# A three-block model on one NeuronCore: delta rule solved by blocks of 64 tokens, pairs of heads taken by turns, zero-filled keys

## The chip, the cores and the metric

The kernel runs on 1 core of one Trainium2 chip. The metric is the device time of one execution in microseconds; lower is better. Everything is float32, batch 1, 256 tokens, model width 2048.

## The reference, cut to what matters

Three blocks run one after the other on the same 256 tokens: gated convolution with linear attention and memory attention; sparse attention with gating and a feed-forward layer; latent attention (MLA) beside a two-way delta rule (RWKV-7). The change touches three places, the index scores of block 2 and both branches of block 3:

```python
# block 2: index scores, 8 heads of 64, one key head for all of them
s = jnp.einsum('bqhd,bsd->bqhs', qib, ki32)
score = jnp.einsum('bqh,bqhs->bqs', wib * idx_scale, jax.nn.relu(s))

# block 3, MLA: 8 heads, 128 columns of their own and 64 rotary ones, the rotary key shared
s = (jnp.einsum('bqhd,bkhd->bhqk', qn_b, k_nope)
     + jnp.einsum('bqhr,bkr->bhqk', qr_b, k_rope))

# block 3, delta rule: 16 heads of 64, forwards and backwards (d), token by token
sa = jnp.einsum('dbhij,dbhj->dbhi', st, a_t)
st = st * w_t[..., None, :] + sa[..., None] * b_t[..., None, :] + v_t[..., None] * k_t[..., None, :]
y = jnp.einsum('dbhij,dbhj->dbhi', st, r_t)
```

## The kernel before, in words

**The stream.** All large weights come from HBM as one stream of items of 128x512 numbers. `run_stream` (L476) goes through them in order. For each item ScalarE rounds the raw weights to `wh` (float32r), VectorE takes the rest, `wl = raw - wh`, and TensorE adds three products (`wh*xh`, `wl*xh`, `wh*xl`) for each half of the tokens into the two PSUM tiles `acc0` and `acc1`: six matmuls of 512 columns an item, or twelve of 256. The split runs five items ahead (`LEAD`).

**The side work.** All else (attention, delta rule, norms, transposes) is written as generators, which `pump` (L425) steps between the stream's matmuls; what TensorE makes for them goes into four further PSUM banks, called `bank` in the rows. A clock inside the builder, `Issue` (L261), has a fixed cost for each instruction; with it `pump` decides at build time after which stream matmul the next step of a generator stands. On the chip each engine then goes through its list in that order, and a TensorE instruction that must wait holds up the whole stream. All instructions pass through one recording line, so rows of the profile read L285, and are told apart by tile names.

**Narrow matmuls.** Heads are 64 wide, so two heads lie one above the other in the 128 partitions. A matmul for one head contracts over 64 partitions (rows `64*128`), and the solver below works on squares of 32 tokens (rows `32*32`, with an explicit `tile_position`). The stream and most side work contract over all 128 (rows `128*128`). A float32 matmul outside the stream stands as two records in the trace.

**Block 2, index scores.** `ev_ki` (L1555) has the key, 64 wide, doubled side by side and transposed into `kiT`, so that it lies in both halves; `indexer` (L1566) makes 8 steps of two matmuls of 64 rows.

**Block 3, MLA.** `ev_kr` (L1959) does the same with the rotary key `krT`. `mla_block` (L2026) adds for each head a product over 128 rows (`qn`, `kn`) and one over 64 rows (both in the slot `ropes`): 16 such pairs in all, each with the narrow matmul behind the full one.

**Block 3, delta rule.** Two jobs, `job(0)` and then `job(1)` (L2191), with 8 heads each; the second starts when the first has been solved. Per job and direction d, with the tokens in two blocks b of 128:
- `scores` (L2445): a matrix per head and block, `ab`, from `bk` and `ar`, 64 rows each; four matmuls a step, all of the same half of the partitions.
- `products` (L2467): 32 steps, each with one head, block and direction: one matmul of 128 columns and one of 256, 64 rows each. VectorE masks the results, and every second step TensorE multiplies three of them with the values (tile `vy`), 128 rows.
- `inverses` (L2517): the 32x32 blocks on the diagonal of `ab` go through DRAM into another layout, VectorE inverts 128 of them at a time, and they come back as `tl`.
- `solve` (L2581): for each of two blocks n, four stages e of 32 tokens, both directions together: 16 matmuls with the inverses (`bank<-w,tl`), ScalarE copies to `w0`, then the later tokens' rows of `ab` times the result (`bank<-w,ab`; 48, 32 and 16 matmuls for e = 0, 1, 2, the first two in two steps each), and VectorE adds. 40 steps and 640 matmuls over both jobs.
- `outputs` (L2689): the last reads (`bank<-w,m`), a norm per head on VectorE and ScalarE, and for the second job the transposes (`bank<-cst,vy`) that give the stream's next matrix, `br1`, its left operand.

Of the kernel before, what the change touches and what calls it, by code (L numbers as in the profile page):

```python
# [15 lines left out]
ALU = mybir.AluOpType  # L16
# [623 lines left out]
class Kernel(Builder):  # L640
# [866 lines left out]
    def block2(self):  # L1507
        nc, B = self.nc, self
        V, A, T, G = nc.vector, nc.scalar, nc.tensor, nc.gpsimd
        cv = self.cv  # L1510
        S = {}
# [24 lines left out]
        def to_T(e, dst, flag, n=4):  # L1536
# [8 lines left out]
            B.flag(flag)  # L1545

        def ev_qi(j, acc):
            S["qi_s"] = B.slot([128, 2048], name="qi")
            S["qiT"] = S["qi_s"][:, :1024].rearrange("p (c t) -> p c t", t=256)
            S["kiT"] = S["qi_s"][:, 1024:1280].rearrange("p (c t) -> p c t", t=256)  # L1550
            S["sc"] = S["qi_s"][:, 1280:1792].rearrange("p (b t) -> p b t", t=256)
            B.scaled(S["qiT"], acc, "Rb2")
            B.flag_then("qiT")

        def ev_ki(j, acc):  # L1555
            e = B.work([128, 256], "nar", 1).rearrange("p (b t) -> p b t", b=2)
            for i in range(2):
                ev_copy(e, acc, 64, 64 * i)
            for b in range(2):
                V.tensor_scalar(out=wi[:, b], in0=acc[b][:, 64:72], scalar1=R[:, b:b + 1], scalar2=512.0 ** -0.5,  # L1560
                                op0=ALU.mult, op1=ALU.mult)
            B.side(to_T(e, S["kiT"], "kiT", 1), True)
            B.side(bias())
            B.side(indexer())

        def indexer():  # L1566
# [3 lines left out]
            for h0 in (0, 4, 1, 5):  # L1570
                p0 = 64 * (h0 % 2)
# [321 lines left out]
    def block3(self):  # L1893
# [3 lines left out]
        S = {}  # L1897
# [61 lines left out]
        def ev_kr(j, acc):  # L1959
            d = B.work([128, 256], "nar", 1).rearrange("p (b t) -> p b t", b=2)  # L1960
            ev_copy(d, acc, R, 64)
            S["qrT"] = S["ropes"][:, :1024].rearrange("p (c t) -> p c t", t=256)
            S["krT"] = S["ropes"][:, 1024:1280].rearrange("p (c t) -> p c t", t=256)

            def g():
                yield from B.lock("mix")
                for b in range(2):
                    rotary(d[:, b:b + 1, 0:64], 1, b)
                    V.tensor_copy(out=d[:, b, 64:128], in_=d[:, b, 0:64])
                B.unlock("mix")  # L1970
                yield from to_T(d, S["krT"], "krT", 1)
            B.side(g(), True)
# [53 lines left out]
        def mla_block(b, i0, mp):  # L2026
# [5 lines left out]
            for h0 in (i0, i0 + 4):  # L2032
                hs = (h0, h0 + 2)
                p0 = 64 * (h0 % 2)
# [410 lines left out]
        def scores(J, d, bk):  # L2445

            ab = J["ab"][d] = yield from B.slotw([128, 16, 128], "ab")
            av = ab.rearrange("p (h b) t -> p h b t", b=2)
            for b in (0, 1) if d == 0 else (1, 0):
                for h0 in range(2):  # L2450
                    ps, = yield from B.bank()
                    for i in range(4):
                        p, c, ar = at(J, d, b, 2 * i + h0)
                        T.matmul(ps[:, i * 128:i * 128 + 128], bk[p, 0, c, b * 128:b * 128 + 128], ar[:, 0],
                                 start=True, stop=True)
                    yield
                    A.copy(out=av[:, h0::2, b], in_=ps.rearrange("p (i t) -> p i t", t=128))
                    B.unbank(ps)
            J["bk"][d] = bk
# [7 lines left out]
        def products(J):  # L2467


            masks = [B.masks[:, d * 256:d * 256 + 256] for d in range(2)]  # L2470
            seq = [(b, h, d) for b in range(2) for h in range(8) for d in range(2)]
            pend, ready = deque(), deque()
            wy, ms, rb = None, [None, None], [None, None]
            for step in range(35):
                if pend:
                    b, h, d, ps = pend.popleft()
                    m = ms[d] = B.work([128, 2, 128], f"m{d}", 3)
                    if h % 2 == 0:
                        rb[d] = B.work([128, 2, 128], f"rb{d}", 2)
                    V.tensor_tensor(out=m.rearrange("p a t -> p (a t)"), in0=ps[:, :256], in1=masks[d], op=ALU.mult)  # L2480
                    V.tensor_tensor(out=rb[d][:, h % 2], in0=ps[:, 256:384], in1=masks[d][:, :128], op=ALU.mult)
                    B.unbank(ps)
                    if h % 2:
                        B.store(J["rbd"][d][:, 8 * b + h - 1:8 * b + h + 1], rb[d])
                    if d:
                        V.tensor_tensor(out=ms[0][:, 0], in0=ms[0][:, 0], in1=m[:, 0], op=ALU.add)
                        ready.append((step, b, h, ms[0], m))
                out = None
                if ready and ready[0][0] < step:
                    _, b, h, m0, m1 = ready.popleft()  # L2490
                    if h % 2 == 0:
                        wy, = yield from B.bank()
                    vs = J["V"][:, b, h * 64:h * 64 + 64]
                    for i, l in enumerate((m0[:, 0], m0[:, 1], m1[:, 1])):
                        o = i * 128 + h % 2 * 64
                        T.matmul(wy[:, o:o + 64], l, vs, start=True, stop=True)
                    if h % 2:
                        out = wy, b, (h - 1) * 64
                if step < 32:
                    b, h, d = seq[step]  # L2500
                    ps, = yield from B.bank()
                    p, c, ar = at(J, d, b, h)
# [3 lines left out]
                    pend.append((b, h, d, ps))  # L2506
                yield
# [9 lines left out]
        def inverses(J):  # L2517
# [54 lines left out]
            for d in (1, 0):  # L2572
                for q in range(4):
                    nc.sync.dma_start(out=ts[32 * q:32 * q + 32, d], in_=td2[d, :, q].rearrange("u c t -> c u t"))
            yield
            V.transpose(out=tb[:, 1], in_=ts[:, 1])
            B.free(tmp)
            J["tt"] = [ts[:, 0], tb[:, 1]]
            B.flag(f"inv{g}")

        def solve(J):  # L2581


            for d in range(2):
                yield from B.wait(f"zb{d}{J['g']}")
            ab, tt, w0, zb = J["ab"], J["tt"], J["w0"], J["zb"]
            pw = yield from B.bank(2)
            hs = [slice(h * 64, h * 64 + 64) for h in range(8)]
            for n in range(2):
                bs = (n, 1 - n)  # L2590
                if n:
                    for c in range(4):
                        for d in range(2):
                            T.matmul(pw[d][:, c * 128:c * 128 + 128], J["ar"][1][:, d, c, 0], zb[d][:, c], start=c == 0,
                                     stop=False, skip_group_check=True)
                for e in range(4):
                    qs = (e, 3 - e)
                    rows = [slice(32 * q, 32 * q + 32) for q in qs]
                    ws = [w0[rows[d], d, bs[d]] for d in range(2)]
# [14 lines left out]

                    for h in range(8 if e < 3 else 0):
                        if h == 4 and e < 2:
                            yield
                        for i in range(e + 1, 4):
                            for d in range(2):
                                t0 = 32 * (i, 3 - i)[d]  # L2620
                                T.matmul(pw[d][t0:t0 + 32, hs[h]], ab[d][rows[d], 2 * h + bs[d], t0:t0 + 32],
                                         ws[d][:, hs[h]], start=not n and e == 0 and h == 0, stop=e == 2,
                                         tile_position=(32 * qs[d], t0), skip_group_check=True)
                if n == 0:
# [361 lines left out]
```

## Time and profile before

| | |
|---|---|
| runs | 3606.69 us median of 3 (3601.64 to 3608.61) |
| the profiled execution | 3603.35 us, its span on the core 3601.6 us |
| granted TensorE clock | 0.995 |
| busy: TensorE, VectorE, ScalarE, GpSimd | 99%, 68%, 53%, 4% |
| chain that ended last | TensorE 97% |

TensorE is the engine that is never free: its matmuls are pipelined, so what one costs is read from the start of one to the start of the next, and not from its duration. A side step costs the stream the time by which the matmuls of the stream on both sides of it stand further apart than without it.

### The profile page before, as it was taken

How to read it: one execution, taken by the hardware profiler on the slowest of the kernel's cores; microseconds unless marked ns; L12 is line 12 of the kernel's file. 1: busy time of each engine (PE TensorE's matmuls, PEld its weight loads, DVE VectorE, ACT ScalarE, POOL GpSimd, SP SyncE). 2: the span in 40 equal slices, each digit the busy share in tenths (PEclk: the TensorE clock that was granted, in tenths of full speed). 3: DMA queues.
4: the chain of work that ended last, by engine and by line, in shares of the span. 5: the costliest groups of instructions: out<-in, count | busy, mean ns of one | idle time of the engine just before them, and what ended most of it. 6: DMA issues, size and time to landing. Idle time of an engine off the chain costs nothing.

```text
span 3601.6 us, 56526 instructions
## 1 busy us (share of the span) xinstructions
PE 3561.6 (99%) x20754; PEld 3063.9 (85%) x20754; DVE 2451.2 (68%) x4453; ACT 1896.3 (53%) x3402; POOL 149.0 (4%) x141
## 2 busy tenths in 40 slices
PE   8999999999999999999999999999999999999988
PEld 7889988888988899888879898989888987887767
DVE  7598888886576665555866555555665688587675
ACT  6555556656554545655455544444564653463334
POOL 1000010010000000000200000000000010000000
PEclk9999999999999999999999999999999999999999
DMA  6555556676677765566665555555663655555655
GB/s 236 169 188 157 182 169 197 208 224 187 195 226 222 239 201 179 187 216 217 232 210 182 191 187 190 188 188 187 198 206 115 196 189 182 193 192 170 199 177 186
DMA packets 231774, 698.51 MB, mean 194 GB/s; under 512 B 40708, under 2 KB 51124, under 8 KB 229832
## 3 DMA queue, kind: packets, MB, share of 16 engines
q1 hardware_dynamic: 231496, 694.90, 59.9%
q8 instruction: 162, 2.65, 0.3%
q14 instruction: 116, 0.95, 0.1%
HBM read 661.22 MB, written 36.73 MB: 194 GB/s over the span
## 4 chain that ended last, share of the span: by engine, by line
PE 97%; DVE 1%; DMA 1%; ACT 0%; issue 0%; SPq 0%; DVEq 0%; ACTq 0%
PE acc L285 87%; PE bank L285 10%; DVE wl L285 0%; DMA raw<-in_wstream_dram 0%; DMA x<-f 0%; ACT wh L285 0%; DVE vy L285 0%; DVE o L285 0%; DVE xl L285 0%; DVE rsz L285 0%; ACT junk L285 0%; DVE yst L285 0%; ACT xh L285 0%; DVE x L285 0%; SPq L285 0%
## 5 line engine op out<-in xcount | busy, mean ns | idle before, releaser
L285 DVE TENSOR_TENSOR wl<-raw,wh 128x512 fp32r<-128x512 f32 x2290 | 1569.6, 701 | 1037.1 <-ACT wh L285 1021.4
L285 ACT ACTIVATE wh<-raw 128x512 fp32r<-128x512 f32 x2290 | 1424.3, 629 | 1529.5 <-PE acc L285 975.8
L285 PE MATMUL acc<-wh,xh 128*128 128x512 f32 x3328 | 1327.0, 399 | 7.3 <-ACT xh L285 4.4
L285 PE MATMUL acc<-wh,xl 128*128 128x512 f32 x3328 | 1298.0, 390 | 3.4 <-DVE xl L285 3.4
L285 PE MATMUL acc<-wl,xh 128*128 128x512 f32 x3328 | 1297.1, 390 | 0.0
L285 PEld LDWEIGHTS acc<-wh,xh 128*128 128x128 f32 x3328 | 626.2, 188 | 154.9 <-issue 20.6
L285 PEld LDWEIGHTS acc<-wh,xl 128*128 128x128 f32 x3328 | 626.0, 188 | 135.6 <-DVE xl L285 4.0
L285 PEld LDWEIGHTS acc<-wl,xh 128*128 128x128 f32 x3328 | 626.9, 188 | 121.8 <-DVE wl L285 0.8
L285 PE MATMUL acc<-xh,wh 128*128 128x256 f32 (+3 forms) x2224 | 638.0, 287 | 0.0
L285 PE MATMUL acc<-xh,wl 128*128 128x256 f32 (+3 forms) x2224 | 630.3, 283 | 0.0
L285 PE MATMUL acc<-xl,wh 128*128 128x256 f32 (+3 forms) x2224 | 630.2, 283 | 0.0
L285 PEld LDWEIGHTS acc<-xh,wh 128*128 128x128 f32 (+3 forms) x2224 | 424.3, 191 | 5.5 <-issue 4.0
L285 PEld LDWEIGHTS acc<-xl,wh 128*128 128x128 f32 (+3 forms) x2224 | 424.5, 191 | 1.1
L285 PEld LDWEIGHTS acc<-xh,wl 128*128 128x128 f32 (+3 forms) x2224 | 424.1, 191 | 0.3
L285 DVE SCALAR_TENSOR_TENSOR cacc<-u,cvec,cacc 128x226 f32<-128x226 f32 (+28 forms) x464 | 188.4, 467 | 0.0
L285 PE MATMUL bank<-ar,bk 64*128 64x128 f32 (+1 forms) x384 | 77.4, 328 | 0.0
L285 PEld LDWEIGHTS bank<-ar,bk 64*128 64x128 f32 x384 | 48.6, 187 | 19.2 <-issue 13.4
L285 ACT ACT_TABLE_LOAD x44 | 56.5, 1283 | 3.2 <-DVE mmx L285 1.6
L285 POOL TENSOR_TENSOR msh<-ev 128x508 f32<-128x508 f32 x8 | 10.8, 1346 | 1038.7 <-DVE ev L285 976.3
L285 ACT ACTIVATE junk<-x 128x512 bf16<-128x512 f32 x40 | 25.3, 631 | 36.7 <-DVE x L285 36.3
L285 PE MATMUL acc<-wh,yr 128*128 128x512 f32 x128 | 44.0, 408 | 0.0
L285 POOL TENSOR_TENSOR crstd<-crstd,u 128x256 f32<-128x256 f32 x14 | 21.8, 1560 | 358.6 <-DVE u L285 358.1
(420 smaller groups left out, 2223.8 us busy)
## 6 DMA issues: line engine op xcount, KB each, us to landing
raw<-in_wstream_dram SPq DMA_DIRECT2D x1133, 512.0 KB, 3.9
gate<-sg SPq DMA_DIRECT2D x40, 256.0 KB, 2.2
row<-in_rows_dram SPq DMA_DIRECT2D x38, 256.0 KB, 4.7
sg<-gate SPq DMA_DIRECT2D x24, 256.0 KB, 2.9
sg<-z SPq DMA_DIRECT2D x24, 256.0 KB, 2.6
z<-sg SPq DMA_DIRECT2D x20, 256.0 KB, 2.1
f<-x SPq DMA_DIRECT2D x16, 256.0 KB, 2.5
gt<-gate SPq DMA_DIRECT2D x16, 256.0 KB, 4.1
```

What stands on the lines that cost most here:

```text
L285: r = f(*a, **k)
```

## The change

**Keys filled with zeros (index scores, MLA).** `kiT` and `krT` now exist twice: once with the key in the upper 64 partitions and zeros in the lower, once the other way round. GpSimd writes the zeros. The matmuls take all 128 rows of the two heads' queries against the version of the head wanted.

**Heads by turns (scores, products).** A step takes two banks and works on the two heads of a pair in turn, one in the upper 64 partitions and one in the lower. `scores` has 2 steps a direction in place of 4, with 8 matmuls; `products` has 16 steps with matmuls in place of 32, with 4 in each.

**Blocks of 64 (inverses, solve).** When the inverses of 32 are back, TensorE joins two of them to one of 64: for a pair of blocks f and s, the block between them times one inverse, a copy, and that times the other. These are 128 matmuls of 32x32x32 a job, in four steps of 32, on four squares of the array by turns. The inverses are laid into `ab` itself: one direction by four further DMAs, the other by four transposes; the joined block by four ScalarE copies, the zeros opposite by GpSimd. `solve` then has two stages of 64 tokens in place of four of 32: three steps of 16 matmuls for each n, so 12 steps and 192 matmuls over both jobs.

The core of the diff:

```diff
+        def halves_T(e, dst, flag):
+            yield
+            t = yield from B.transposes([e[:, b] for b in range(2)], 128)
+            yield
+            for i in range(2):
+                V.tensor_copy(out=dst[64 * i:64 * i + 64, i], in_=t[64 * i:64 * i + 64, :256])
...
+            for i in range(2):
+                G.memset(S["kiT"][64 - 64 * i:128 - 64 * i, i], 0.0)
...
-                        T.matmul(ps[:, i * n:i * n + n], S["qiT"][p0:p0 + 64, h0 // 2 + i, b * 128:b * 128 + 128],
-                                 S["kiT"][p0:p0 + 64, 0, :n], start=True, stop=True)
+                        T.matmul(ps[:, i * n:i * n + n], S["qiT"][:, h0 // 2 + i, b * 128:b * 128 + 128],
+                                 S["kiT"][:, h0 % 2, :n], start=True, stop=True)
...
-                    T.matmul(o, S["qrT"][p0:p0 + 64, h // 2, tb], S["krT"][p0:p0 + 64, 0], start=False, stop=True)
+                    T.matmul(o, S["qrT"][:, h // 2, tb], S["krT"][h0 % 2], start=False, stop=True)
...  scores
-                for h0 in range(2):
-                    ps, = yield from B.bank()
-                    for i in range(4):
-                        p, c, ar = at(J, d, b, 2 * i + h0)
-                        T.matmul(ps[:, i * 128:i * 128 + 128], bk[p, 0, c, b * 128:b * 128 + 128], ar[:, 0],
-                                 start=True, stop=True)
+                ps = yield from B.bank(2)
+                for i in range(4):
+                    for h0 in range(2):
+                        p, c, ar = at(J, d, b, 2 * i + h0)
+                        T.matmul(ps[h0][:, i * 128:i * 128 + 128], bk[p, 0, c, b * 128:b * 128 + 128], ar[:, 0],
+                                 start=True, stop=True)
...  products
-                    T.matmul(ps[:, 256:384], J["bk"][d][p, 0, c, ts], ar[:, 1], start=True, stop=True)
-                    T.matmul(ps[:, :256], J["bk"][d][p, 1, c, ts], ar[:, ::-1], start=True, stop=True)
+                    for i, (p, _, ar) in enumerate(hs):
+                        T.matmul(ps[i][:, 256:384], J["bk"][d][p, 0, c, ts], ar[:, 1], start=True, stop=True)
+                    for i, (p, _, ar) in enumerate(hs):
+                        T.matmul(ps[i][:, :256], J["bk"][d][p, 1, c, ts], ar[:, ::-1], start=True, stop=True)
...  inverses
+            for q, qs in enumerate(qss):
+                nc.sync.dma_start(out=ab[0][qs, :, qs], in_=td2[0, :, q].rearrange("u c t -> c u t"))
...
+            for qs in qss:
+                V.transpose(out=ab[1][qs, :, qs], in_=ts[qs, 1])
+            V.transpose(out=tb[:, 0], in_=ts[:, 0])
...
+            prs = [(d, qss[2 * i + d], qss[2 * i + 1 - d], 32 * (2 * i + d), 32 * (2 * i + 1 - d))
+                   for i in range(2) for d in range(2)]
+            flipped = [tb[:, 0], ts[:, 1]]
+            zt, = yield from B.bank()
+            for u in range(16):
+                for d, f, s, tf, t2 in prs:
+                    T.matmul(zt[s, u * 32:u * 32 + 32], ab[d][f, u, s], flipped[d][f, u], start=True, stop=True,
+                             tile_position=(tf, t2), skip_group_check=True)
+                if u == 7:
+                    yield
+            yield
+            zs = tb[:, 1]
+            A.copy(out=zs.rearrange("p u t -> p (u t)"), in_=zt)
...  the second product alike, from zs and ab into zt
+            for d, f, s, _, _ in prs:
+                A.copy(out=ab[d][f, :, s], in_=zt[f].rearrange("p (u t) -> p u t", t=32))
+                G.memset(ab[d][s, :, f], 0.0)
...  solve
-                for e in range(4):
-                    qs = (e, 3 - e)
-                    rows = [slice(32 * q, 32 * q + 32) for q in qs]
+                for e in range(2):
+                    os = (64 * e, 64 - 64 * e)
+                    rows = [slice(o, o + 64) for o in os]
...
-                            T.matmul(pw[d][rows[d], hs[h]], tt[d][rows[d], 2 * h + bs[d]], ws[d][:, hs[h]], start=True,
-                                     stop=True, tile_position=(32 * qs[d], 32 * qs[d]), skip_group_check=True)
+                            T.matmul(pw[d][rows[d], hs[h]], ab[d][rows[d], 2 * h + bs[d], rows[d]], ws[d][:, hs[h]],
+                                     start=True, stop=True, tile_position=(os[d], os[d]), skip_group_check=True)
...
-                    for h in range(8 if e < 3 else 0):
...
+                    for h in range(8 if e == 0 else 0):
+                        for d in range(2):
+                            o = os[1 - d]
+                            T.matmul(pw[d][o:o + 64, hs[h]], ab[d][rows[d], 2 * h + bs[d], o:o + 64], ws[d][:, hs[h]],
+                                     start=not n, stop=True, tile_position=(os[d], o), skip_group_check=True)
```

How this moves instructions shows at three places. The first is TensorE's list in `products` of the first job; `bank_N<-ar,bk` are the products of a step, into the bank with that number. Before, one step, the stream, the next step:

```order
L285 MATMUL bank_30314<-ar,bk 128x128
L285 MATMUL bank_30314<-ar,bk 128x256
L285 MATMUL acc_30095<-wh,xh 128x512
L285 MATMUL acc_30095<-wl,xh 128x512
L285 MATMUL acc_30095<-wh,xl 128x512
L285 MATMUL bank_30331<-ar,bk 128x128
L285 MATMUL bank_30331<-ar,bk 128x256
```

Now one step, with two banks in turn:

```order
L285 MATMUL bank_30168<-ar,bk 128x128
L285 MATMUL bank_30169<-ar,bk 128x128
L285 MATMUL bank_30168<-ar,bk 128x256
L285 MATMUL bank_30169<-ar,bk 128x256
L285 MATMUL acc_30093<-wh,xh 128x512
L285 MATMUL acc_30093<-wl,xh 128x512
L285 MATMUL acc_30093<-wh,xl 128x512
```

What stood in two steps with a piece of the stream between them stands in one step.

The second place is TensorE's list at the end of the second job, from the last reads (`w,m`) to the transposes of the result (`cst,vy`). Before, 27 matmuls of the stream stand between them, of which the first and the last are shown:

```order
L285 MATMUL bank_34933<-w_32295,m_34027 128x64 x8
L285 MATMUL acc_34864<-wh,yr_33886 128x512
...
L285 MATMUL acc_34962<-wh,yr_33886 128x512
L285 MATMUL bank_35054<-cst_80,vy 128x128 x4
L285 MATMUL bank_35061<-cst_80,vy 128x128 x4
L285 MATMUL acc_35068<-wh,yr_35052 128x512
```

Now 108 matmuls of the stream stand between the reads and the first transposes, and 6 more before the second:

```order
L285 MATMUL bank_34560<-w_32123,m_34060 128x64 x8
...
L285 MATMUL acc_34821<-wh,yr_33946 128x512
L285 MATMUL bank_34844<-cst_80,vy 128x128 x4
L285 MATMUL acc_34820<-wh,yr_33946 128x512
L285 MATMUL acc_34820<-wl,yr_33946 128x512
...
L285 MATMUL bank_34861<-cst_80,vy 128x128 x4
```

The reads have moved up in the stream by 93 matmuls, and the transposes, which come just before `br1`, by 12 and by 6.

The third place is ScalarE's list at the end of `inverses` of the first job, where all is new; `wh` is the stream's split, `w` the solver's copy:

```order
L285 COPY tl<-bank_31132 128x512
L285 ACTIVATE wh<-raw 128x512
L285 COPY ab<-bank_31220 32x16x32
L285 COPY ab<-bank_31220 32x16x32 x3
L285 ACTIVATE wh<-raw 128x512
L285 COPY w_29037<-bank_31322 64x512
```

The first copy lies between the two products of the joining, the four after it between the joining and the first step of `solve`. On TensorE's list 9 matmuls of the stream cover each of the two in the first job, 9 and 12 in the second.

## Rows read from the trace of the kernel before

**Rows 1.** The page: busy time, chain by line, VectorE's largest group

```profile
PE 3561.6 (99%) x20754; PEld 3063.9 (85%) x20754; DVE 2451.2 (68%) x4453; ACT 1896.3 (53%) x3402; POOL 149.0 (4%) x141
...
PE acc L285 87%; PE bank L285 10%; DVE wl L285 0%; DMA raw<-in_wstream_dram 0%; DMA x<-f 0%; ACT wh L285 0%; DVE vy L285 0%; DVE o L285 0%; DVE xl L285 0%; DVE rsz L285 0%; ACT junk L285 0%; DVE yst L285 0%; ACT xh L285 0%; DVE x L285 0%; SPq L285 0%
...
L285 DVE TENSOR_TENSOR wl<-raw,wh 128x512 fp32r<-128x512 f32 x2290 | 1569.6, 701 | 1037.1 <-ACT wh L285 1021.4
```

**Rows 2.** TensorE's waits: who for whom, us in total, times, longest

```profile
PE bank L285 <- DVE vy L285: 16.2, 1, 16.2
```

**Rows 3.** Timeline of TensorE, a full-form step: start, us, engine, line, what

```profile
1407.22 0.28 PE L285 MATMUL acc<-xh,wl 128*128 128x256 f32 x1
1407.34 1.05 PE L285 MATMUL bank<-kv,apT 128*128 128x128 f32 x8
...
1408.34 0.28 PE L285 MATMUL acc<-xl,wh 128*128 128x256 f32 x1
```

**Rows 4.** Timeline of TensorE, a step of scores and one of products

```profile
2933.58 0.39 PE L285 MATMUL acc<-wh,xl 128*128 128x512 f32 x1
2933.90 1.16 PE L285 MATMUL bank<-ar,bk 64*128 64x128 f32 x8
...
2935.32 0.39 PE L285 MATMUL acc<-wl,xh 128*128 128x512 f32 x1
2935.55 0.40 PE L285 MATMUL acc<-wh,xl 128*128 128x512 f32 x1
...
2952.12 0.40 PE L285 MATMUL acc<-wh,xl 128*128 128x512 f32 x1
2952.45 0.92 PE L285 MATMUL bank<-ar,bk 64*128 64x128 f32 x4
...
2953.63 0.40 PE L285 MATMUL acc<-wl,xh 128*128 128x512 f32 x1
```

**Rows 5.** Timeline of TensorE, steps of solve in the first job

```profile
3066.92 0.39 PE L285 MATMUL acc<-wh,xl 128*128 128x512 f32 x1
3067.24 1.08 PE L285 MATMUL bank<-w,tl 32*32 32x64 f32 x32
...
3068.59 0.39 PE L285 MATMUL acc<-wl,xh 128*128 128x512 f32 x1
...
3071.21 0.73 PE L285 MATMUL bank<-w,ab 32*32 32x64 f32 x48
...
3081.73 0.65 PE L285 MATMUL bank<-w,ab 32*32 32x64 f32 x32
...
3090.70 1.08 PE L285 MATMUL bank<-w,ab 32*32 32x64 f32 x32
```

**Rows 6.** Timeline of TensorE, the pairs of MLA

```profile
2748.22 0.70 PE L285 MATMUL bank<-ropes 64*128 64x256 f32 x2
2748.85 0.70 PE L285 MATMUL bank<-kn,qn 128*128 128x256 f32 x2
2749.48 0.70 PE L285 MATMUL bank<-ropes 64*128 64x256 f32 x2
```

**Rows 7.** TensorE's groups by form: records, busy us, mean ns, idle before

```profile
L285 PE MATMUL bank<-ar,bk 64*128 64x128 f32 x256 | 49.6, 304 | 0.0
L285 PE MATMUL bank<-ar,bk 64*128 64x256 f32 x128 | 38.1, 377 | 0.0
```

**Rows 8.** Timeline of TensorE at the end of the second job

```profile
3448.25 3.68 PE L285 MATMUL bank<-w,m 128*128 128x64 f32 x32
3451.73 0.48 PE L285 MATMUL acc<-wh,yr 128*128 128x512 f32 x1
...
3474.50 1.94 PE L285 MATMUL bank<-cst,vy 128*128 128x128 f32 x8 [16.20 <-DVE vy L285]
```

**Rows 9.** Busy us of each engine in 44 us of products

```profile
2966.00:3010.00 44.00, 44.00 (x205) 33.70 (x204) 39.53 (x85) 17.20 (x30) 1.28 (x1) 1.00 0.59 193
```

**Rows 10.** ScalarE's groups from 3066 to 3152: the solver's copies

```profile
L285 ACT COPY w<-bank 32x512 f32<-32x512 f32 x16 | 9.2, 578 | 5.8 <-PE bank L285 5.5
```

More of the change, by code (lines that the diff above doesn't have):

```diff
@@ L1545, in to_T @@
             B.flag(flag)
+        def halves_T(e, dst, flag):
[4 more added lines that the diff above has]
+                V.tensor_copy(out=dst[64 * i:64 * i + 64, i], in_=t[64 * i:64 * i + 64, :256])
+            B.unbank(t)
+            B.flag(flag)
         def ev_qi(j, acc):
@@ L1561, in ev_ki @@
                                 op0=ALU.mult, op1=ALU.mult)
-            B.side(to_T(e, S["kiT"], "kiT", 1), True)
+            B.side(halves_T(e, S["kiT"], "kiT"), True)
             B.side(bias())
@@ L1570, in indexer @@
             for h0 in (0, 4, 1, 5):
-                p0 = 64 * (h0 % 2)
                 for b in range(2):
@@ L1962, in ev_kr @@
             S["qrT"] = S["ropes"][:, :1024].rearrange("p (c t) -> p c t", t=256)
-            S["krT"] = S["ropes"][:, 1024:1280].rearrange("p (c t) -> p c t", t=256)
+            S["krT"] = [S["ropes"][:, o:o + 256] for o in (1024, 1792)]
+            for i in range(2):
+                G.memset(S["krT"][i][64 - 64 * i:128 - 64 * i], 0.0)
             def g():
@@ L1970, in g @@
                 B.unlock("mix")
-                yield from to_T(d, S["krT"], "krT", 1)
+                yield
+                t = yield from B.transposes([d[:, b] for b in range(2)], 128)
+                yield
+                for i in range(2):
+                    V.tensor_copy(out=S["krT"][i][64 * i:64 * i + 64], in_=t[64 * i:64 * i + 64, :256])
+                B.unbank(t)
+                B.flag("krT")
             B.side(g(), True)
@@ L2470, in products @@
             masks = [B.masks[:, d * 256:d * 256 + 256] for d in range(2)]
-            seq = [(b, h, d) for b in range(2) for h in range(8) for d in range(2)]
+            seq = [(b, c, d) for b in range(2) for c in range(4) for d in range(2)]
             pend, ready = deque(), deque()
-            wy, ms, rb = None, [None, None], [None, None]
-            for step in range(35):
+            m0 = None
+            for step in range(19):
                 if pend:
[L2476 to L2484, printed above, removed]
-                    if d:
-                        V.tensor_tensor(out=ms[0][:, 0], in0=ms[0][:, 0], in1=m[:, 0], op=ALU.add)
-                        ready.append((step, b, h, ms[0], m))
@@ new lines, in products @@
+                    b, c, d, ps = pend.popleft()
+                    m = [B.work([128, 2, 128], f"m{d}{i}", 2 - d) for i in range(2)]
+                    rb = B.work([128, 2, 128], f"rb{d}", 2)
+                    for i in range(2):
+                        V.tensor_tensor(out=m[i].rearrange("p a t -> p (a t)"), in0=ps[i][:, :256], in1=masks[d], op=ALU.mult)
+                        V.tensor_tensor(out=rb[:, i], in0=ps[i][:, 256:384], in1=masks[d][:, :128], op=ALU.mult)
+                    B.unbank(*ps)
@@ L2488, in products @@
+                    B.store(J["rbd"][d][:, 8 * b + 2 * c:8 * b + 2 * c + 2], rb)
+                    if d:
+                        for i in range(2):
+                            V.tensor_tensor(out=m0[i][:, 0], in0=m0[i][:, 0], in1=m[i][:, 0], op=ALU.add)
+                        ready.append((step, b, c, m0, m))
+                    else:
+                        m0 = m
                 out = None
                 if ready and ready[0][0] < step:
-                    _, b, h, m0, m1 = ready.popleft()
@@ L2491, in products @@
[L2491 to L2502, printed above, removed]
-                    ts = slice(b * 128, b * 128 + 128)
-                    T.matmul(ps[:, 256:384], J["bk"][d][p, 0, c, ts], ar[:, 1], start=True, stop=True)
-                    T.matmul(ps[:, :256], J["bk"][d][p, 1, c, ts], ar[:, ::-1], start=True, stop=True)
-                    pend.append((b, h, d, ps))
+                    _, b, c, ms, mt = ready.popleft()
@@ new lines, in products @@
+                    wy, = yield from B.bank()
+                    for i in range(2):
+                        vs = J["V"][:, b, c * 128 + i * 64:c * 128 + i * 64 + 64]
+                        for a, l in enumerate((ms[i][:, 0], ms[i][:, 1], mt[i][:, 1])):
+                            o = a * 128 + i * 64
+                            T.matmul(wy[:, o:o + 64], l, vs, start=True, stop=True)
+                    out = wy, b, c * 128
+                if step < 16:
+                    b, c, d = seq[step]
+                    ps = yield from B.bank(2)
+                    ts = slice(b * 128, b * 128 + 128)
+                    hs = [at(J, d, b, 2 * c + i) for i in range(2)]
+                    for i, (p, _, ar) in enumerate(hs):
+                        T.matmul(ps[i][:, 256:384], J["bk"][d][p, 0, c, ts], ar[:, 1], start=True, stop=True)
+                    for i, (p, _, ar) in enumerate(hs):
+                        T.matmul(ps[i][:, :256], J["bk"][d][p, 1, c, ts], ar[:, ::-1], start=True, stop=True)
+                    pend.append((b, c, d, ps))
@@ L2585, in solve @@
                 yield from B.wait(f"zb{d}{J['g']}")
-            ab, tt, w0, zb = J["ab"], J["tt"], J["w0"], J["zb"]
+            ab, w0, zb = J["ab"], J["w0"], J["zb"]
             pw = yield from B.bank(2)
@@ L2613, in solve @@
                     yield
-                    for h in range(8 if e < 3 else 0):
[L2616 to L2623, printed above, removed]
+                    for h in range(8 if e == 0 else 0):
[3 more added lines that the diff above has]
+                                     start=not n, stop=True, tile_position=(os[d], o), skip_group_check=True)
                 if n == 0:
```

31 lines of the change are left out of this document (21 added, 10 removed).

## The prediction

> **What bounds the kernel now.** I read the page first: TensorE is busy 99% of the span, and by line the chain of waits is 87% matmuls of the stream into `acc` and 10% side work into `bank`; VectorE's largest group is the stream's split, 701 ns each [rows 1]. Then who waited for whom: TensorE's only long wait is 16.2 us, once, for VectorE's `vy` [rows 2]. So a microsecond of side work on TensorE is a microsecond of the kernel, as long as what it needs comes in time. Then the timeline, for what a side step costs the stream: from the start of the last stream matmul before it to the start of the second after it, less the two paces that would lie there anyway (0.12 us each at 256 columns, 0.23 at 512).
>
> Three readings carry the sum.
>
> *A full-form step.* Four matmuls of 128 rows and 128 columns: 1408.34 - 1407.22 - 0.24 = 0.88 us, 0.22 each, with nothing for entering or leaving [rows 3].
>
> *A narrow step.* The same four with 64 rows: 2935.32 - 2933.58 - 0.46 = 1.28, that is 0.40 more [rows 4]. The step of `products` with one matmul of 128 and one of 256 columns takes 2953.63 - 2952.12 - 0.46 = 1.05, so 0.40 + 0.22 + 0.43. The surcharge is thus paid per step, about 0.20 on each side, whatever stands in it. MLA shows it bare: full and narrow matmuls follow each other every 0.63 us [rows 6], 0.20 over the 0.43 that 256 columns take.
>
> *Squares by turns.* A step of 16 matmuls on two squares of 32x32 takes 3068.59 - 3066.92 - 0.46 = 1.21, its row's length plus 0.13 [rows 5]. Less 0.40 that is 0.81 for eight matmuls a square, 0.10 each on its own square, the other square beside it. The 24 matmuls on six squares take 0.73 + 0.13 = 0.86, less 0.40 that is 0.46 or 0.019 each; they share rows of the array and, in different banks, columns, and still run side by side. The 16 on four squares take 0.65 + 0.13 = 0.78.
>
> **The change part by part.**
>
> *Index scores.* Eight narrow steps become full: 8 x 0.40 = -3.2 us. The zeros are four GpSimd writes, here and in MLA, on an engine busy 4% [rows 1]; nothing.
>
> *MLA.* 16 pairs, two changes of form each: 32 x 0.20 = -6.4.
>
> *Scores.* Before 16 steps (128 of the records, so 64 matmuls [rows 7]) of 1.28. After, 8 steps with four matmuls in either half of the rows. I take the halves to run side by side, since squares with distinct rows and shared columns do [rows 5]: 8 x 1.28, -10.2. From above, one behind the other: 8 x (0.40 + 8 x 0.22) = 17.3, -3.2. Below the first there is nothing, for each half needs its four passes.
>
> *Products.* 64 steps of 1.05 (the other 128 records of 128 columns and the 128 of 256 [rows 7]) become 32. Side by side: -33.6. One behind the other: 32 x (0.40 + 2 x 0.65) = 54.4, -12.8. The products with the values stay 96 full matmuls.
>
> *Solve.* Before, for each of four (two jobs, two n): four steps of 1.21, two of 0.86, two of 0.78, one of 1.21 [rows 5], 9.33; together 37.3. After, 12 steps of 16 matmuls on two squares of 64x64. The moved columns are 64 as before, so I take 1.21 each: 14.5, -22.8. If the two squares did not overlap, 16 x 0.10 + 0.40 = 2.0 each, -13.3; below 1.21 a square would have to take fewer passes, which it doesn't.
>
> *Inverses.* Eight new steps of 32 matmuls on four squares, 32 columns each. No row shows 32 columns. From below half of 0.10 a matmul on its square, 8 x 0.05 + 0.40 = 0.80, together 6.4; from above all in a row at 0.10, 3.6, together 28.8. I take the pace of the six squares, 32 x 0.019 + 0.40 = 1.01, the nearest in number and kind: +8.1. The four DMAs and four transposes a job stand behind the same kind of work and before the reads of it; VectorE and the DMA queue have that time, since they finish while `products` still runs.
>
> The Trainium skill, page "TensorE: Matmul & The Clock Gate", section "Wait — 56ns, not 53.3ns?", says that matmuls start at least about 25 ns apart however few columns they have. By it an inverse step, with 64 records, would take 1.6 + 0.4 us and the eight some 16 (an estimate from that page), and the forecast would be 8 us later. The trace differs: 48 records start within 0.46 us, about 10 ns apart, on six squares [rows 5]; I go by the row.
>
> Sum on TensorE: -3.2 - 6.4 - 10.2 - 33.6 - 22.8 + 8.1 = -68.1 us.
>
> *The wait at the end of job 1.* The last reads end at 3451.73, the transposes begin at 3474.50, 22.8 us later [rows 8]. Of these 6.2 were covered by 27 stream matmuls at 0.23, the rest is the wait. In the new order 108 stand between, 24.8 us. But VectorE's list now has 13 splits and two pairs of products from `acc` among the norm's instructions, and had 4 and one pair: 9 x 0.70 [rows 1] and 2 x 0.70, 7.7 us more. So 22.8 + 7.7 - 24.8 = 5.7 us of wait stay of 16.2: -10.5. From below none stays, if VectorE works through the gaps it had; from above all 16.2.
>
> *What is late next.* After joining, four ScalarE copies at 0.58 [rows 10], 2.3 us and some latency, meet a cover of 9 matmuls (2.1 us) in job 0 and 12 in job 1; behind them stands the first step of `solve`, and the stream behind that: +0.5. In the densest stretch of `products` VectorE is busy 39.5 of 44 us [rows 9]; with ten steps in it made five, at 1.05, the stretch would be 38.7 long, below VectorE's own work: I take 2.5 us for both jobs. Together +3, from 0 to the 20 of the second rival.
>
> All: -68.1 - 10.5 + 3 = -75.6, against the profiled execution's 3603.35: 3527.8. That execution lies 3.3 below the median of the runs, 3606.69; I add half of it and forecast 3530 us.
>
> **The rivals.**
>
> *Halves one behind the other.* Two heads in the upper and lower 64 rows each use all 128 columns, which no row before shows; the squares by turns [rows 5] speak for overlap, at 32 rows only. Then scores and products save 3.2 and 12.8: TensorE -40.3, with the rest -47.8, 3556 to 3557.
>
> *VectorE takes over.* If the share of the dense stretch, 0.90 [rows 9], held from the first scores to the first step of `solve`, 2933.6 to 3067.2 [rows 4, 5], that stretch of 134 us could shrink by 13.4 and not by 21.9 (scores and products of one job): 17 us come back over two jobs, and with VectorE behind, the wait at the end keeps its 16.2. 3527.8 + 17 + 10.5 is 3555. For it: `products` brings VectorE the same masking in less time. Against it: TensorE waited for nothing there [rows 2], and the new order spreads the steps further apart.
>
> *Each turn of halves costs a change of form, and the kernel gets slower.* The surcharge of 0.20 a side [rows 6] might fall due at each turn between the two halves of the rows. There are 8 x 7 turns in scores, 32 x 3 in products, 12 x 15 in solve, 332. Nothing would overlap there: products -12.8, scores -3.2, solve -13.3, inverses +8.1, keys -9.6, -30.8; with 332 x 0.20 = +66.4 and -7.5 for the waits the kernel takes 3631. It decides from 0.12 us a turn. Against it: 16 matmuls by turns on squares with distinct rows take 0.81 us, in which 15 turns at 0.20 would be 3.0 [rows 5].
>
> **How the numbers follow.** Forecast 0.72, with a range of its own from 3515 (no wait at the end, the cheapest inverses, no new waits) to 3548 (the wait stays, dearer inverses). Halves in a row 0.12, VectorE 0.11, dear turns 0.05. To hold 8 in 10 I go up to the first two rivals: 3514 to 3558. A measurement of this kernel tells 0.2%, some 7 us, from no change. All cases but the last are far beyond that; for mixtures that eat up the gain I leave 0.02 for the same: faster 0.93, same 0.02, slower 0.05.
>
> **What would show it.** A step of `products` with four matmuls at about 1.05 us, one of `scores` with eight at 1.28; at 1.7 and 2.2 the halves take turns in earnest. A step of `solve` at 1.21, of the joining at 1.0. MLA's matmuls every 0.43. The wait for `vy` at a third of 16.2, and no wait of over 2 us between scores and solve. The forecast is wrong if these steps cost as said and TensorE's list of waits holds more than some 15 us that is new, or if the halves don't overlap.

## The result

The changed kernel takes 3540.87 us (median of 4, 3537.31 to 3546.78) against 3605.53 us before (4 runs): ratio 0.9823, 95% interval 0.9805 to 0.9841. It is 64.7 us faster; 75.6 were forecast. The time lies inside the range, 11 us above the forecast of 3530.

The profiled execution after took 3546.78 us, 5.9 above its median, and is 56.6 below the profiled one before. The page after, the busy row of its first part:

```profile
PE 3506.3 (99%) x20370; PEld 3036.2 (86%) x20370; DVE 2442.9 (69%) x4447; ACT 1893.6 (53%) x3398; POOL 158.8 (4%) x153
```

TensorE is as full as in [rows 1]. What differs stands in the list of its waits (who for whom, us in total, times, longest), against [rows 2]:

```profile
PE acc L285 <- issue: 3.6, 1, 3.6
...
PE acc L285 <- DVE yr L285: 2.0, 2, 1.8
PE bank L285 <- issue: 1.9, 2, 1.8
...
PE bank L285 <- DVE m L285: 1.3, 1, 1.3
PE bank L285 <- ACT w L285: 1.2, 1, 1.2
PE acc L285 <- DVE wl L285: 1.2, 3, 0.8
...
PE bank L285 <- DVE tl L285: 0.6, 1, 0.6
```

The one wait of 16.2 us for `vy` is gone. In its place stand eleven short ones, 11.8 us in these rows, and two lines of them have no releaser ("issue"); a further new one, 0.8 us for `qi`, stands in the index scores.

The steps themselves, from the timeline of TensorE after (start, us, engine, line, what), in order: MLA, a step of scores, one of products, one of the joining, one of solve:

```profile
2743.01 0.60 PE L285 MATMUL bank<-kn,qn 128*128 128x256 f32 x2
2743.44 0.59 PE L285 MATMUL bank<-ropes 128*128 128x256 f32 x2
...
2930.39 0.39 PE L285 MATMUL acc<-wh,xl 128*128 128x512 f32 x1
2930.71 1.16 PE L285 MATMUL bank<-ar,bk 64*128 64x128 f32 x16
...
2932.14 0.39 PE L285 MATMUL acc<-wl,xh 128*128 128x512 f32 x1
...
2943.40 0.40 PE L285 MATMUL acc<-wh,xl 128*128 128x512 f32 x1
2943.72 0.93 PE L285 MATMUL bank<-ar,bk 64*128 64x128 f32 x8
...
2944.91 0.39 PE L285 MATMUL acc<-wl,xh 128*128 128x512 f32 x1
...
3049.86 0.40 PE L285 MATMUL acc<-wh,xl 128*128 128x512 f32 x1
3050.19 0.75 PE L285 MATMUL bank<-ab,tl 32*32 32x32 f32 x64
...
3051.21 0.40 PE L285 MATMUL acc<-wl,xh 128*128 128x512 f32 x1
...
3344.21 0.39 PE L285 MATMUL acc<-wh,xl 128*128 128x512 f32 x1
3344.53 1.15 PE L285 MATMUL bank<-w,ab 64*64 64x64 f32 x32
...
3345.94 0.39 PE L285 MATMUL acc<-wl,xh 128*128 128x512 f32 x1
```

Read as in the prediction, less 0.46 or twice 0.23: scores 1.29 for eight matmuls [rows 4: 1.28 for four], products 1.05 for four (1.05 for two), joining 0.89, solve 1.27 (the median of the twelve is 1.28), MLA 0.43 a matmul [rows 6: 0.63 for a pair's turn].

**Where the microseconds stand.** Both traces have the same 17,208 matmuls of the stream in the same order. So the start of each in one trace can be set against its start in the other; the table sums by how much the time between two such marks changed, in us, for the profile after and for a second profile of the same kernel (`after_again`, run 3542.99). The last two columns belong to an experiment below.

| stretch of the stream | after | again | spread | spread again |
|---|---|---|---|---|
| parts that the change doesn't touch, up to MLA | +3.6 | +1.1 | -0.8 | +4.5 |
| index scores | -1.9 | -1.9 | -1.9 | -1.6 |
| MLA to the first scores | -4.7 | -6.2 | -6.2 | -4.7 |
| scores and products, first job | -15.5 | -15.2 | -17.6 | -17.0 |
| joining of the first job | +6.5 | +6.5 | -0.2 | 0.0 |
| solve, then the second job's scores and products | -14.9 | -16.3 | -14.0 | -11.4 |
| joining and solve, second job | -9.0 | -7.8 | -4.0 | -3.5 |
| last reads, transposes | -20.5 | -20.4 | -21.9 | -21.5 |

But for the first, the stretches repeat within some 1.5 us in the two profiles of the changed kernel (once 2.6 in the two of the spread one). The joining of the first job alone costs 6.5 us more than what stood there before, and most of that is a halt:

```profile
3051.44 0.39 PE L285 MATMUL acc<-wh,xl 128*128 128x512 f32 x1
3055.44 0.59 PE L285 MATMUL acc<-wh,xh 128*128 128x512 f32 x1 [3.60 <-issue]
3055.82 0.63 PE L285 MATMUL acc<-wl,xh 128*128 128x512 f32 x1
```

When the matmul at 3055.44 begins, TensorE has finished 2024 items of the stream and VectorE has split 2030. The split of the item that TensorE comes to is the first of these three, done at 3045.98, so its data had been there for 9 us:

```profile
3045.29 1.89 DVE L285 TENSOR_TENSOR wl<-raw,wh 128x512 fp32r<-128x512 f32 x3
```

The DMA queues in that gap, 3051.4 to 3055.4 (packets, MB, share of the 16 engines' time):

```profile
q1 hardware_dynamic: 517, 1.45, 100.6%
q8 instruction: 1, 0.02, 1.5%
```

One piece of instructions, 16 KB, moves from 3053.23 to 3054.17, beside queues that data fill. Over the whole kernel this queue moves 159 pieces for TensorE's 2 x 20370 records, one for every 256. My reading is that TensorE had come to the end of what it had loaded: just before, it went through two blocks of 256 records in 4.4 and 2.8 us, where the five before these had taken 17 to 27 us each. The piece begins to move only 1.4 us after TensorE has stopped; why so late, no run tells. And the halt has a tail. The stretches behind it, columns as in [rows 9] (PEclk is the granted clock):

```profile
3055.40:3058.10 2.70, 2.66 (x8) 1.62 (x7) 0.00 (x0) 0.00 (x0) 0.00 (x0) 0.50 1.07 408
3059.20:3062.00 2.80, 2.80 (x16) 2.33 (x13) 0.78 (x2) 1.79 (x3) 0.00 (x0) 1.00 1.02 423
```

After this halt TensorE is granted half its clock (0.50), 1.2 of 2.4 GHz: six matmuls of the stream start 0.43 apart in place of 0.23, 1.2 us more.

### The profile page after: what moved, and what is told of

It reads as the page before. It is cut to its first block, busy times and chain, and to the rows that moved or that the text cites. A ratio compares the mean times of both kernels' runs of the same rounds, so it can differ in the third digit from the quotient of the medians.

```text
span 3545.0 us, 55751 instructions
## 1 busy us (share of the span) xinstructions
PE 3506.3 (99%) x20370; PEld 3036.2 (86%) x20370; DVE 2442.9 (69%) x4447; ACT 1893.6 (53%) x3398; POOL 158.8 (4%) x153
## 4 chain that ended last, share of the span: by engine, by line
PE 91%; DVE 5%; DMA 2%; issue 1%; ACT 1%; SPq 0%; POOL 0%; DVEq 0%; ACTq 0%
PE acc L285 84%; PE bank L285 7%; DVE wl L285 2%; DVE tmp L285 1%; DMA raw<-in_wstream_dram 1%; DVE m L285 0%; ACT wh L285 0%; DMA x<-f 0%; DMA tl<-td 0%; DVE tl L285 0%; DVE rb L285 0%; ACT junk L285 0%; DVE o L285 0%; DVE xl L285 0%; DMA row<-in_rows_dram 0%
## 5 line engine op out<-in xcount | busy, mean ns | idle before, releaser
L285 PE MATMUL acc<-wh,yr 128*128 128x512 f32 x128 | 43.7, 410 | 2.0 <-DVE yr L285 2.0
L285 PE MATMUL bank<-ar,bk 64*128 64x128 f32 (+1 forms) x384 | 40.4, 329 | 0.1
L285 POOL TENSOR_TENSOR crstd<-crstd,u 128x256 f32<-128x256 f32 x14 | 21.9, 1561 | 356.5 <-DVE u L285 356.0
L285 PEld LDWEIGHTS bank<-ar,bk 64*128 64x128 f32 x384 | 25.6, 186 | 14.2 <-issue 10.0
```

The source lines that it names most:

```text
L285: r = f(*a, **k)
```

## The experiments

**One part at a time.** Each is the kernel before with one of the three parts of the diff shown above, and nothing else.

> The kernel before with the zero-filled keys alone (index scores and MLA). Theory A (every step of TensorE costs what it cost in the prediction, and what is missing of the forecast went into new short waits of the joining and the solver): eight narrow steps and 32 changes of form go, 3.2 + 6.4 = 9.6 us less, about 3596 us; in the profile MLA's matmuls follow every 0.43 us and the wait for vy at the end stays at 16.2 us. Theory B (full rows move more and the writes of zeros or the contention for SBUF eat it up): under 4 us less.

Measured: 3595.49 us against 3607.45, ratio 0.9971 (0.9960 to 0.9982), 12.0 us less, with 9.6 inside the interval. `vy` is waited for 16.2 us as before. Theory A holds.

> The kernel before with the heads by turns alone (scores and products). Theory A: scores 8 x 1.30 in place of 16 x 1.29, products 32 x 1.06 in place of 64 x 1.05, together 43.7 us less. The list of TensorE has 27 matmuls of the stream between the last reads of the second job and their transposes as before, so the wait of 16.2 us for vy stays: about 3562 us, and up to 3 more for a wait for VectorE's masks in the dense stretch. Theory B (the shorter products leave VectorE behind, and the end waits longer): the wait for vy above 20 us and 3570 us or more.

Measured: 3572.90 us, ratio 0.9907 (0.9893 to 0.9920), 34.6 us less and not 43.7. Its waits:

```profile
PE bank L285 <- DVE vy L285: 16.2, 1, 16.2
...
PE bank L285 <- DVE w L285: 2.8, 2, 2.3
```

The time is one that theory B named, but not for its reason: the wait at the end stays at 16.2, as theory A said, and the steps cost 1.05 and 1.29. But the solver's first step, still of 32, now waits for VectorE, and seven matmuls behind it run at half clock (1.4 us); seven steps of products, waiting inside for their second bank, take 1.18 to 1.71 in place of 1.05 (2.6 us together). The matmuls with the values, three before and six a step now, take 1.35 a step where two steps beside narrow ones had taken 0.62 each (16 x 0.11 = 1.8 us). 2.8 + 1.4 + 2.6 + 1.8 are 8.6 of the 9.1 us missing.

> The kernel before with the blocks of 64 alone (inverses and solve). Theory A: solve 12 x 1.28 in place of 37.4 us, -22; eight joining steps at 0.9, +7; 120 matmuls of the stream now stand between the last reads and the transposes, so the wait for vy goes, -16.2 and 2 us at half clock behind it; and TensorE stands still for some 3 to 7 us in the joining, without a releaser, while 16 KB of its instructions are fetched: -26 to -30, 3575 to 3580 us. Theory B (the stall in the joining belongs to the three parts together, to VectorE's or ScalarE's backlog): no idle time of over 1 us in the joining, -33, about 3572 us.

Measured: 3574.10 us, ratio 0.9908 (0.9894 to 0.9921), 33.3 us less. Theory B's number came true: no halt in the joining, where steps of `products` still stood among those of the joining, so that the first job's four steps take 9.0 us and not 7.0; and the wait at the end is this part's to remove, but for a rest:

```profile
PE bank L285 <- DVE vy L285: 2.7, 1, 2.7
```

The three parts alone save 12.0 + 34.6 + 33.3 = 79.9 us, together 64.7. Some 15 us are lost where they meet; by the intervals of the four ratios this difference is good to about 10 us.

**Is the halt a lack of instructions?** In the first job alone the two halves of each product of the joining are set 18 matmuls of the stream apart:

```diff
                 if u == 7:
-                    yield
+                    for _ in range(1 if g else 6):
+                        yield
```

> The changed kernel with 18 matmuls of the stream in place of 3 between the two halves of each product of the joining, in the first job alone. Theory A (TensorE ran out of fetched instructions: four steps of 128 within 8 us): the idle 3.6 us before the first step of solve and the half clock of six matmuls behind it, 1.4 us, are gone or under 1 us together, about 5 us less than the changed kernel, so 0.14% lower in its ratio to the kernel before. Theory C (the idle time is a wait that the profile doesn't name, for ScalarE's four copies or a bank): the copies stand as close before solve as they did, the idle time stays at 3 to 4 us and the time is the same within 2 us.

Measured: 3534.72 us, ratio 0.9799 (0.9786 to 0.9813). The first job's stretch went from +6.5 to -0.2 (table). In the second job, where nothing was spread, the halt stayed, and at the same place: at record 38337 of TensorE's list, as in the changed kernel, whose first-job halt is at 35009, just 13 x 256 before. The waits of `spread`:

```profile
PE bank L285 <- issue: 2.7, 1, 2.7
...
PE bank L285 <- DMA x<-in_lora_dram: 1.3, 2, 0.7
```

> The changed kernel with each matmul of the joining made twice in a row, so eight steps of 64 matmuls. Theory A (the list of TensorE is fetched in pieces of 16 KB, and a step of 256 instructions within 1.2 us outruns that): beside 8 x 0.44 = 3.5 us for the matmuls, four more pieces a job must come within the joining, with one or more further halts of 2 to 6 us in each job: 12 to 25 us more than the changed kernel, and each halt ends when a piece of 16 KB has landed. Theory C (the halt is a wait on another engine): 3 to 5 us more, and no further halt.

Measured: 3556.87 us, ratio 0.9859 (0.9844 to 0.9874), 13 (by the ratios) to 16 us (by the medians) more than the changed kernel. TensorE's waits without a releaser sum to 13.2 us; those of the first job:

```profile
3042.81 1.15 PE L285 MATMUL bank<-tl,ab 32*32 32x32 f32 x112 [2.41 <-issue]
...
3049.40 1.23 PE L285 MATMUL bank<-ab,tl 32*32 32x32 f32 x122 [1.41 <-issue]
...
3055.07 1.17 PE L285 MATMUL bank<-ab,tl 32*32 32x32 f32 x70 [2.91 <-issue]
```

Three halts a job. They end at records 34753, 35009, 35265 and 38849, 39105, 39617 of the list, each a multiple of 256 from the others, and 1.2 to 1.6 us after a piece has landed. No wait on another engine would fall on such places, so theory C is out. (The pieces that came in addition are two a job, 163 in place of 159 in all, and not four a job.)

A halt doesn't need DMA queues that are full while it lasts. Two of those in the second job, of 1.92 and 1.87 us, end at 3329.01 and 3338.70, and beside them the queues are all but idle; whether data before them made the pieces late, no run tells. From 3326.4 to 3329.0:

```profile
q1 hardware_dynamic: 34, 0.09, 8.7%
q8 instruction: 1, 0.02, 2.3%
```

**Where does the gain of spreading go?** Spreading in the second job too:

```diff
                 if u == 7:
-                    yield
+                    for _ in range(2 if g else 6):     # first product; 1 if g else 6 in the second
+                        yield
```

> The kernel with the joining of the first job spread, and in the second job six matmuls of the stream in place of three between the halves of the first product. The second job's halt of 2.9 us should shrink to 0 to 2. But its last reads move back by 18 matmuls, 4.1 us, so 90 of 108 are left before the transposes. Theory A (the end of the second job is on the path, and VectorE there has no slack left): the wait for vy and yr grows by 2 to 5 us, and the time is the same as with the first job spread alone or up to 3 more, 3534 to 3538. Theory B (there is slack at the end): 2 to 3 us less, 3532.

Measured: 3547.59 us, ratio 0.9833 (0.9819 to 0.9848), 13 us above `spread` and not 0 to 3, but only 7.5 above the second measurement of that kernel (`spread_again`, below), whose interval overlaps this one. The second job's halt is down to 1.4, but the transposes again wait:

```profile
PE bank L285 <- DVE vy L285: 8.1, 2, 6.1
```

Theory A had the direction, not the size. The reads move back by 18 matmuls of the stream (4.1 us), the transposes by 12 and 6, so 102 stand between and not 90; yet 8.1 us of waiting for `vy` return, while the 2.0 for `yr` go. Both transposes now stand together (as before the change), so that, as I read it, the wait for the first also takes away the stream that covered the second; that was not tried by itself.

> The changed kernel once more, beside the next two on the same chip: 3541 us within 4, ratio to the kernel before 0.982; in the profile a halt of TensorE without a releaser in the joining of each job, at the same places of its list as before.

> The kernel with the first job's joining spread once more, to tell its time from the changed kernel's. Theory A (the halt of 3.6 us and the half clock of six matmuls behind it are saved, the second job's halt stays): 5 us less than the changed kernel, 3536. Theory C (the difference of the first measurement was scatter): within 2 us of it.

Measured side by side: 3539.43 (ratio 0.9816, 0.9802 to 0.9829) and 3540.10 (0.9821, 0.9808 to 0.9835): the same. Both profiles of the changed kernel have the halt at record 35009, both of the spread one have none there; yet over the two comparisons the spread kernel is 6.1 us faster once (by medians not measured side by side) and 0.7 slower once. The table shows where it goes: of the 6.5 us, about 3 return in the stretch behind (1 and 5 in the two pairs), with a wait for `x<-in_lora_dram` of 1.1 to 1.3 that is new, and 4 to 5 in the second job's joining, whose halt grows from 1.8 and 2.3 to 2.7 and 3.5. That TensorE lacks instructions at the halt is settled; whether the spread kernel is faster is not.

> The kernel with the first job's joining spread, and the 64 additions of the masked products (128x128) on GpSimd in place of VectorE. Theory A (VectorE is the late one in the dense stretch and at the end: the waits for m, rb, wl and yr are its backlog): 64 additions of some 0.2 us less on VectorE, the builder's order moves the second job's last reads 54 matmuls up in the stream, waits for m, wl and yr together 3 to 6 us less than with the joining spread alone, 3529 to 3532. Theory B (GpSimd is slower per element and TensorE waits for the added m instead): a wait for m of GpSimd in each of 32 steps, some 0.5 us, 10 us or more above, 3545.

```diff
-                            V.tensor_tensor(out=m0[i][:, 0], in0=m0[i][:, 0], in1=m[i][:, 0], op=ALU.add)
+                            G.tensor_tensor(out=m0[i][:, 0], in0=m0[i][:, 0], in1=m[i][:, 0], op=ALU.add)
```

Measured: 3535.50 us, ratio 0.9806 (0.9792 to 0.9819), overlapping that of the changed kernel beside it, so not told apart. The wait for `yr` (2.0 in `spread`) is gone and that for `wl` is down from 2.5 to 0.5; `m` had no wait in `spread` either. Another took their place:

```profile
PE bank L285 <- DVE rb L285: 5.1, 6, 2.1
```

It fits VectorE's backlog as the cause of those waits, though the reads also stand 54 matmuls earlier here; it doesn't make a kernel that is shown to be faster.

**Do the halves run side by side, and does it take turns?**

> The changed kernel with both heads of a pair read from the upper 64 partitions, so that the odd head's products are those of the even one (part of the computation is changed); banks, order and number of instructions stay. Theory A (the two heads run side by side because they lie in different rows of the array): a step of scores becomes 0.40 + 8 x 0.22 = 2.16 in place of 1.30 us, one of products 0.40 + 2 x 0.65 = 1.70 in place of 1.06, 8 x 0.86 + 32 x 0.64 = 27 us more than the changed kernel, about 3568. Theory B (the saving is that a step with its change of form serves two heads, and the overlap comes from two banks): the same time as the changed kernel within 4 us.

```diff
-            p = slice(64 * (h % 2), 64 * (h % 2) + 64)
+            p = slice(0, 64)
```

Measured: 3560.41 us, ratio 0.9869 (0.9853 to 0.9886), 17 to 20 us above the changed kernel (ratios, medians). A step of products:

```profile
2945.70 0.40 PE L285 MATMUL acc<-wh,xl 128*128 128x512 f32 x1
2946.03 1.57 PE L285 MATMUL bank<-ar,bk 64*128 64x128 f32 x8
...
2947.87 0.40 PE L285 MATMUL acc<-wl,xh 128*128 128x512 f32 x1
```

1.71 against 1.05, and 2.18 against 1.29 in scores: theory A's steps, to 0.02 us. Not all of 27 us show. Slower products give VectorE time, and TensorE's waits are 4.4 us shorter here, with none for `m`; the rest is not accounted for.

> The changed kernel with the heads of a pair one after the other within the step: in scores four matmuls of the even head and then four of the odd one, in products both of the even head and then both of the odd one. Theory A (TensorE begins matmuls in the order of its list, so only neighbours in different halves overlap): a step of scores about 1.9 and one of products about 1.5 us, 18 to 25 us more than the changed kernel, some 3560. Theory B (each half has a queue of its own, and the turns don't matter): steps at 1.30 and 1.06 and the same time within 4 us.

```diff
-                for i in range(4):
-                    for h0 in range(2):
+                for h0 in range(2):
+                    for i in range(4):
```

(in `scores`; in `products` the loop over the second matmul is joined to the first). Measured: 3545.55 us, ratio 0.9829 (0.9814 to 0.9844), 2 to 5 us above, within the noise; the steps decide. One of scores and one of products:

```profile
2923.73 0.39 PE L285 MATMUL acc<-wh,xl 128*128 128x512 f32 x1
2924.05 1.71 PE L285 MATMUL bank<-ar,bk 64*128 64x128 f32 x16
...
2926.02 0.39 PE L285 MATMUL acc<-wl,xh 128*128 128x512 f32 x1
...
2938.61 0.40 PE L285 MATMUL acc<-wh,xl 128*128 128x512 f32 x1
2938.94 0.93 PE L285 MATMUL bank<-ar,bk 64*128 64x128 f32 x8
...
2940.14 0.39 PE L285 MATMUL acc<-wl,xh 128*128 128x512 f32 x1
```

Scores 1.83, about as theory A had it; products 1.07, as theory B had it. Neither is whole. Record by record: in products the second half's first record starts 13 ns after the first half's first, past three records that stand ahead of it; in scores 6 ns after the first half's fifth of eight, again past three. So in both steps a matmul of the other half of the rows overtakes three records and no more, and in these two turns are needed only where a half has more than four records in a row.

## Why the prediction was right, and where it was 11 us off

- *The surcharge per step, and MLA's pairs.* Held: by what side steps push the stream aside, index scores -1.9 for -3.2 (with a new wait of 0.8 for `qi`), MLA -6.3 for -6.4 (in one of the two profiles 1.5 come back before the first scores).
- *Scores and products, halves side by side.* The steps held, 1.29 and 1.05, and `same_half` shows the overlap. The gain was short: by what the steps push the stream aside, -38.6 for -43.8 with the full steps among them, for a wait for `m` (1.3), the values' matmuls (1.8) and slow products (1.6); a wait for `w` (1.2) and half clock behind the one for `m` (1.4) come on top.
- *Dear turns.* Refuted: in a step by turns the two halves' records start 6 ns apart.
- *Solve.* -21.9 for -22.8: a step takes 1.28 where I took 1.21.
- *Inverses.* Bare 8 x 0.89 = 7.1 for 8.1. The page "TensorE: Matmul & The Clock Gate" of the Trainium skill has a floor of 25 ns between starts (section "Wait — 56ns, not 53.3ns?"), by which a step would take 1.6 us before the change of form (an estimate from that page). It doesn't hold on these four squares: the 64 records of a step start within 0.56 us, about 9 ns apart. (The 48 records of [rows 5], for which the prediction has 0.46 us by its sum, start within 0.52.)
- *The wait at the end.* 5.7 us were to stay; none did at the transposes, the lower bound. Two short ones for `yr`, which I hadn't named, cost 2.0 and some half clock. The removal is the work of the shorter solver: 16.2 stay in `turns_only`, 2.7 in `blocks_only`.
- *What is late next: "+3, from 0 to the 20".* This step failed, in size and in kind. Of the waits in the list 6.3 us are VectorE's and ScalarE's, as the second rival had it in small; 5.5 are TensorE's own, out of instructions, which no term held. And three of the five pauses of over a microsecond have six to nine matmuls at half clock behind them, 0.2 us each, which I left out.

So the 11 us are partly luck: the end gave back 5.7 us more than forecast, less the 2.0 for `yr`, and so covered a part of the new waits. The prediction's own sign of being wrong, steps that cost as said and more than some 15 us of new waits, was just about reached: the whole list holds 14.6 us that is new, and 15.5 in the second profile of the kernel.

That halt the Trainium skill would have warned of only in part: "Runtime: NRT & Kernel Launch", section "Instruction fetch mechanics", says that lists are fetched in blocks of 16 KiB, 256 instructions, while the block before runs, and that crossing into one is mostly hidden. The size agrees with 159 pieces here. It wasn't hidden where two blocks in a row went by in 4.4 and 2.8 us, and was in the first job of `spread` (5.5 and 7.6) and of `blocks_only` (3.4, then 12.7).

## What to carry to other kernels

Price side work per step, by its change of form, and fill the step; that is what this change does, and the price of steps that the rows showed held to 0.07 us. Then, for each place that gets denser, ask three feeders: the engine that evacuates, the engine that splits, and TensorE's own instruction list, of which small matmuls eat far more per microsecond (256 records in 2.8 us in the joining, in 17 to 27 before it). A pause of TensorE costs its length and, in three of five here, half clock behind it; and parts that each pay alone (79.9 us) paid less together (64.7). I take it that each had lived on slack that the others use up; the runs show that for the halt, which `blocks_only` doesn't have.

## What the runs showed of the hardware that was not expected

- TensorE halted for up to 3.6 us without a releaser, always at list places a multiple of 256 records apart, and went on 1.2 to 1.6 us after a piece of 16 KB had landed (0.9 us of transfer), beside full DMA queues as well as beside idle ones (`join_twice`).
- TensorE does not begin matmuls strictly in the order of its list, as I had written of the engines: with different halves of the rows a record starts past three older ones. The Trainium skill ("TensorE: Matmul & The Clock Gate", section "The mechanism") has matmuls in strict order; the records of `half_after_half` differ.
- 32 float32 matmuls of 32x32x32 on four squares, 64 records, start within 0.56 us, about 9 ns apart.
